# Both products of a feed-forward by seven block products, accumulated on one another in PSUM, with the activations' factors parked in DRAM

## The chip, the core and the metric

One core of one Trainium2 chip runs the program. The metric is the device time of one execution in microseconds, as the median of several runs. The profile is of one further execution; its engines are TensorE (PE, with PEld for its weight loads), VectorE (DVE), ScalarE (ACT), GpSimd (POOL) and SyncE (SP, whose queue issues the DMAs).

## What is computed

A trunk of two encoder layers on two requests, 512 and 256 tokens, with 1024 channels. Each layer is a mixer, a cross attention into a memory of 256 tokens, and a gated feed-forward with 2816 inner channels:

```python
def trunk(x, mem, ...):
    for l in range(DEPTH):
        h = rms_norm(x, norm_mix[l])
        ...                                   # even: convolution and Fourier; odd: windowed means
        h = rms_norm(x, norm_xa[l])
        m = rms_norm(mem, norm_mem[l])
        x = x + memory_cross_attn(h, m, xa_wq[l], xa_wkv[l], xa_wo[l])
        h = rms_norm(x, norm_ffn[l])
        x = x + swiglu(h, ffn_w_gate_up[l], ffn_w_down[l])
    return rms_norm(x, norm_final)

def swiglu(h, w_gate_up, w_down):
    gu = h @ w_gate_up
    g, u = gu[..., :D_FF], gu[..., D_FF:]
    return (jax.nn.silu(g) * u) @ w_down
```

Everything is float32.

## The kernel before

The residual stream stays in SBUF for the whole program: eight tiles `x[k]` of 128 channels by 768 tokens. A product in float32 is three matmuls of operands with short mantissas: `split` writes a high part on ScalarE (L119, with a gain L122) and the rest on VectorE (L120, L123), and `prod` multiplies high by high, high by low and low by high. One unit of weights is fetched by SP into one of four tiles `raw` (L138) and split into `wh` and `wl` in a pool of seven.

The feed-forward (`ffn`) goes by chunks of 128 inner channels, 22 of them, in the groups (4, 4, 4, 5, 5). A group's chunks get their gates and values, then its down products are added to x (`residual`, L289). Tokens are handled as halves of 384, so that a matmul is 128x384.

- Chunks 0 to 3 are plain: `linear` for gates and for values, eight input chunks by two token halves by three matmuls each.
- Chunks 4 to 21 use Winograd's form of Strassen's product (`seven`): gates and values are the rows, the two halves of the input channels the inner blocks, the two halves of the tokens the columns. Seven block products of sums of blocks take the place of eight, 7 × 4 × 3 = 84 matmuls a chunk. `left_factors` makes the seven weights' sums and splits them; `right_factors` makes the sums of the normalised input once. The latter is a generator that `advance(rf, PRE)` drives piecewise beside plain chunks 2 and 3 and the first down product. VectorE adds the seven results into gates and values (L871, L872).
- All down products are plain, `linear` over the group's activations, which stay in SBUF.
- In layer 0's last group, `advance(beside, 2)` makes the memory's parts for the mixer of layer 1. In layer 1's last group the down product goes by two pieces of the tokens, so that the final norm of one runs beside the product of the other.

All tiles are in one set of pools for the whole program; each engine's order is the scheduler's, by these dependencies.

## Time and profile before

| | |
|---|---|
| Median of three runs | 1805.79 us (1805.6 to 1805.99) |
| Span of the profiled execution | 1803.7 us |
| TensorE busy | 1785.7 us, 99% |
| VectorE busy | 1311.6 us, 73% |
| ScalarE busy | 668.5 us, 37% |
| Moved by DMA | 130.33 MB, of which 3.15 MB written |

The page gives no time for the profiled execution beyond its span, which runs from its first to its last instruction; the median lies 2.1 us above it. A share on the page is a mean over stages of different kinds. In the rows of the prediction a group has its count, its busy time, the mean of one in ns, and the idle time of the engine ahead of it with what ended it; a row of a stretch has, after its length, each engine's busy time with its number of instructions, the granted clock of TensorE, the share of DMA and GB/s; a row of the chain or the timeline has start and duration in us.

### The profile page before, as it was taken

What the parts mean: (1) busy time and instruction counts of PE and PEld (TensorE: products, weight loads), DVE (VectorE), ACT (ScalarE), POOL (GpSimd) and SP (SyncE); (2) the same over time, 40 slices, a digit from 0 to 9 for tenths busy, and PEclk for the clock granted to TensorE, in tenths of its full rate; (3) what the DMA queues carried; (4) which work ended last, traced back from release to release, by engine and by line L of the source; (5) the groups of instructions that cost most, each with busy time, mean ns of one, the idle gap of its engine ahead of it and who ended that gap; (6) DMA issues with size and microseconds to landing.
All of it is one profiled execution on the core that took longest, in us unless ns stands there. A gap on an engine that the chain in (4) does not pass through costs nothing.

```text
span 1803.7 us, 26005 instructions
## 1 busy us (share of the span) xinstructions
PE 1785.7 (99%) x10606; PEld 1748.0 (97%) x10606; DVE 1311.6 (73%) x2083; ACT 668.5 (37%) x1049; POOL 2.5 (0%) x40
## 2 busy tenths in 40 slices
PE   9999999999999999999999999999999999999997
PEld 8999999999999999999999999999999999999996
DVE  7998976486787757585767984496697767684765
ACT  7233243353443424242345243362443323241341
POOL 0000000000000000000000000000000000000000
PEclk9999999999999999999999999999999999999999
DMA  7231321111112221222224231111113121222211
GB/s 250 82 116 55 95 67 54 47 36 59 53 30 94 59 82 54 87 66 63 71 60 128 82 104 60 36 49 57 47 36 95 57 83 53 87 63 68 78 52 70
DMA packets 44326, 130.33 MB, mean 72 GB/s; under 512 B 4912, under 2 KB 6192, under 8 KB 44208
## 3 DMA queue, kind: packets, MB, share of 16 engines
q1 hardware_dynamic: 44208, 128.68, 23.5%
q8 instruction: 83, 1.36, 0.3%
q14 instruction: 35, 0.29, 0.1%
HBM read 125.51 MB, written 3.15 MB: 71 GB/s over the span
## 4 chain that ended last, share of the span: by engine, by line
PE 97%; DVE 2%; DMA 0%; ACT 0%; SPq 0%; issue 0%; DVEq 0%; ACTq 0%
PE acc L155 97%; DVE s L120 1%; DMA x<-in_x 0%; PE acc L713 0%; DVE s L988 0%; DVE st L695 0%; ACT Rx L234 0%; DVE c L704 0%; DVE kl L120 0%; DVE s L662 0%; SPq L304 0%; DVE x L975 0%; DVE c L221 0%; DVE s L123 0%; ACT s L122 0%
## 5 line engine op out<-in xcount | busy, mean ns | idle before, releaser
L155 PE MATMUL acc<-s,wh 128*128 128x384 f32 (+1 forms) x3528 | 782.4, 339 | 5.1 <-ACT Rx L234 3.6
L155 PEld LDWEIGHTS acc<-s,wh 128*128 128x128 f32 x3528 | 624.6, 188 | 21.4 <-ACT Rx L234 6.1
L155 PE MATMUL acc<-s,w 128*128 128x384 f32 x3120 | 543.8, 334 | 0.0
L155 PEld LDWEIGHTS acc<-s,w 128*128 128x128 f32 x3120 | 541.0, 188 | 0.4
L155 PE MATMUL acc<-s,wl 128*128 128x384 f32 (+1 forms) x1764 | 466.6, 339 | 0.0
L155 PEld LDWEIGHTS acc<-s,wl 128*128 128x128 f32 x1764 | 319.1, 188 | 6.5 <-DVE wl L120 0.5
L119 ACT ACTIVATE wh<-raw 128x1024 fp32r<-128x1024 f32 (+3 forms) x179 | 155.3, 873 | 454.6 <-PE acc L155 427.1
L120 DVE TENSOR_TENSOR wl<-raw,wh 128x1024 fp32r<-128x1024 f32 (+3 forms) x177 | 175.5, 995 | 115.1 <-PE acc L155 87.2
L289 DVE TENSOR_TENSOR x<-acc,x 128x768 f32<-128x768 f32 x152 | 145.1, 956 | 134.5 <-PE acc L155 134.5
L871 DVE TENSOR_TENSOR c<-acc,c 128x384 f32<-128x384 f32 x252 | 133.3, 553 | 43.6 <-PE acc L155 28.3
L119 ACT ACTIVATE w<-raw 128x512 fp32r<-128x512 f32 x148 | 92.5, 630 | 171.9 <-PE acc L155 168.7
L119 ACT ACTIVATE w<-h 128x512 fp32r<-128x512 f32 x108 | 68.1, 632 | 177.9 <-PE acc L155 177.9
L155 PE MATMUL acc<-wh,s 128*128 128x256 f32 x704 | 129.0, 283 | 0.0
L120 DVE TENSOR_TENSOR w<-raw,w 128x512 fp32r<-128x512 f32 x148 | 101.3, 689 | 24.6 <-ACT w L119 24.6
L155 PEld LDWEIGHTS acc<-wh,s 128*128 128x128 f32 x704 | 110.6, 192 | 0.2
L120 DVE TENSOR_TENSOR w<-h,w 128x512 fp32r<-128x512 f32 x108 | 74.1, 687 | 38.3 <-ACT w L119 38.3
L119 ACT ACTIVATE s<-c 128x768 fp32r<-128x768 f32 (+1 forms) x92 | 68.2, 756 | 66.9 <-DVE c L919 19.5
L155 PE MATMUL acc<-wl,s 128*128 128x256 f32 x328 | 92.8, 283 | 0.0
L120 DVE TENSOR_TENSOR s<-c,s 128x768 fp32r<-128x768 f32 (+1 forms) x92 | 76.6, 853 | 15.8 <-ACT s L119 14.6
L155 PE MATMUL acc<-s,s 128*128 128x512 f32 (+3 forms) x492 | 86.6, 334 | 0.0
L155 PEld LDWEIGHTS acc<-s,s 128*128 128x128 f32 x492 | 75.8, 189 | 9.8
L395 DVE SCALAR_TENSOR_TENSOR c<-c,vec,c 128x392 f32<-128x392 f32 x124 | 70.5, 633 | 0.2
(132 smaller groups left out, 1241.7 us busy)
## 6 DMA issues: line engine op xcount, KB each, us to landing
raw<-in_wgu SPq DMA_DIRECT2D x88, 512.0 KB, 3.5
raw<-in_wd SPq DMA_DIRECT2D x48, 256.0 KB, 2.6
raw<-in_wd SPq DMA_DIRECT2D x32, 320.0 KB, 2.9
raw<-in_wk SPq DMA_DIRECT2D x16, 512.0 KB, 3.6
raw<-in_wv SPq DMA_DIRECT2D x16, 512.0 KB, 3.6
raw<-in_wq SPq DMA_DIRECT2D x16, 512.0 KB, 3.5
raw<-in_wo SPq DMA_DIRECT2D x16, 512.0 KB, 3.5
raw<-in_m SPq DMA_DIRECT2D x16, 256.0 KB, 2.7
```

Source lines behind the costliest of these rows:

```text
L119: nc.scalar.activation(hi, src, AF.Copy)
L120: nc.vector.tensor_tensor(lo, src, asf(hi), ALU.subtract)
L155: nc.tensor.matmul(o, a, b, start=start, stop=stop)
L289: nc.vector.tensor_tensor(two(x[d]), halves(ps), two(x[d]), ALU.add)
L395: nc.vector.scalar_tensor_tensor(out_, src[:, a : a + CL], w, prev, ALU.mult, ALU.add)
L871: add = lambda o, a, b: nc.vector.tensor_tensor(o, a, b, ALU.add)
```

## The change

- Chunks 0 and 1 stay plain; chunks 2 to 21 go by seven products.
- The down product goes by seven products too, for two chunks (a pair) and two blocks of 128 output channels at a time: `output_job`. Its groups count pairs: (2, 3, 3, 3) in layer 0, (2, 3, 4) in layer 1, whose last two pairs stay plain and go by pieces of the tokens as before. A group has four output jobs, with 42 matmuls per job for a group of two pairs, 63 for three and 84 for four.
- Both kinds of jobs run through one pipeline, `run`. Results P6, P5 and P3 are accumulated in PSUM on top of P1, and P4 on top of P7. P3 and P4 of a job are made between P1 and P5 of the next. A weight's factor (`left`) is made six products ahead; its sums are on VectorE (L871 to L877). PSUM tiles in the feed-forward are one bank each, eight of them.
- When a pair of chunks is done, `finished` makes its sums and parts at once and parks them in DRAM, 2.75 MB in four writes on SP's queue (`keep`, L921); layer 1's last two pairs write parts alone. `load` reads a group's factors back (L1051): for the first group in the last hidden job, for group g+1 ahead of the weights of group g's second job.
- The input's factors are all made behind the token scale R, around the sums of plain chunks 0 and 1 (`some_factors`, then `other_factors`, L984 and L814).
- The memory's parts for layer 1 are made at the start of `mixer_odd`.
- The pools of mixer and attention (`mixing`) and those of the feed-forward (`feeding`) are separate sets, opened and closed in turn on the same memory.

Line numbers move: `split` is L144 to L148, the fetch L163, the matmul L180, the residual add L320, sums of the feed-forward L813 and L814.

```diff
-GROUPS = (4, 4, 4, 5, 5)
-PLAIN = GROUPS[0]
-PRE = 3
+NPAIR = NF // 2
+GROUPS = ((2, 3, 3, 3), (2, 3, 4))
+AHEAD = 6
...
-    rawp = E(tc.tile_pool(name="rawp", bufs=4))
...
-    acc = E(tc.tile_pool(name="acc", bufs=4, space=bass.MemoryType.PSUM))
+    park = E(tc.tile_pool(name="park", bufs=1, space=bass.MemoryType.DRAM))
...
+            pool = lambda name, bufs, **k: s.enter_context(tc.tile_pool(name=name, bufs=bufs, reuse_waits="tile", **k))
+            rawp, wp, hp, cp, sp = pool("rawp", 4), pool("wp", 7), pool("hp", 3), pool("cp", 8), pool("sp", 19)
+            acc = pool("acc", 4, space=bass.MemoryType.PSUM)
+            yield
...
+            f = SimpleNamespace()
+            rawp, wp, f.sum, f.pair, f.t2 = pool("raw2", 4), pool("wp2", 7), pool("sum", 2), pool("pair", 2), pool("t2", 4)
+            cp, sp = pool("cp2", 4), pool("sp2", 18)
+            acc = pool("acc2", 8, space=bass.MemoryType.PSUM)
+            yield f
...
-    def mixer_odd(l, o, ms):
+    def mixer_odd(l, o):
         hs = split_x(x, "mix", l)
-        ks, vs = [], []
+        ms, ks, vs = [], [], []
+        advance(memory_parts(l, ms), KD)
...
+        def first_factors(r, spare):
+            s1 = duo_split(r[:, 0::2, :])
+            t13 = chunk()
+            sub(two(t13), r[:, 1::2, :], r[:, 0:2, :])
+            s2 = duo_split(two(t13))
+            t2 = fp.t2.tile([P, H], F32, tag="t2", name=nm("t2"))
+            sub(t2, r[:, 3, :], t13[:, :H])
+            th = next(spare)
+            split(th[:, :H], th[:, H:T], t2)
+            return s1, s2, th, t2
...
+        def left(job, role):
+            n = job.cols
+            if role == "P1":
+                if job.before is not None:
+                    job.before()
+                job.a1, job.a2 = [fetch(src, 2 * n) for src in job.src]
+                a21, a22 = job.a2[:, :n], job.a2[:, n : 2 * n]
+                job.s1, job.s2 = [fp.sum.tile([P, 512], F32, tag="sum", name=nm("sum"))[:, :n] for _ in range(2)]
+                put(job, role, job.a1[:, :n])
+                WSUM(job.s1, a21, a22, ALU.add)
+                WSUM(job.s2, job.s1, job.a1[:, :n], ALU.subtract)
+                WSUM(a21, job.a1[:, :n], a21, ALU.subtract)
+            elif role == "P2":
+                a12 = job.a1[:, n : 2 * n]
+                put(job, role, a12)
+                WSUM(a12, a12, job.s2, ALU.subtract)
+            else:
+                src = {"P6": job.s2, "P7": job.a2[:, :n], "P5": job.s1, "P3": job.a1[:, n : 2 * n], "P4": job.a2[:, n : 2 * n]}
+                put(job, role, src[role])
+        def product(job, role):
+            home = {"P6": "P1", "P5": "P1", "P3": "P1", "P4": "P7"}.get(role)
+            if home is None:
+                job.bank[role] = bank()[:, :H]
+            o = job.bank[home or role]
+            w = job.w.pop(role)
+            m = len(job.right)
+            for k, right in enumerate(job.right):
+                prod([o], cut(w, slice(k * P, (k + 1) * P)), [right[role]], k == 0 and home is None, k == m - 1, home is not None)
+            for f in job.on[role]:
+                f(o)
+        def run(jobs):
+            seq, prev = [], None
+            for job in jobs:
+                for role in ("P1", "P2", "-P3", "P6", "-P4", "P7", "P5"):
+                    if role[0] != "-":
+                        seq.append((job, role))
+                    elif prev is not None:
+                        seq.append((prev, role[1:]))
+                prev = job
+            seq += [(prev, "P3"), (prev, "P4")]
+            for i in range(-AHEAD, len(seq)):
+                if i + AHEAD < len(seq):
+                    left(*seq[i + AHEAD])
+                if i >= 0:
+                    product(*seq[i])
...
+    def finished(q, pt):
...
+            d = parked[q] = park.tile([P, 3 * SLOT + T], F32, tag=f"pk{l}_{q}", name=f"pk{l}_{q}")
+            r = four(pt)
+            s1, s2, th, t2 = first_factors(r, spare)
+            sub(r[:, 1, :], r[:, 2, :], t2)
+            s4 = duo_split(r[:, 1::2, :])
+            for i, s in enumerate((s1, s2, s4)):
+                keep(d[:, i * SLOT : (i + 1) * SLOT], s)
+            keep(d[:, 3 * SLOT :], th)
...
+        some_factors(0)
+        act(0, *p0)
+        for k in range(1, M):
+            some_factors(k)
+        act(1, pg, plain(1, 1))
+        right = [other_factors(k) for k in range(M)]
...
+        def load(g):
+            back = lambda t, q, a, n: nc.sync.dma_start(t.bitcast(F32), parked[q][:, a : a + n])
+            got = {}
+            for i in (0, 3, 1, 2):
+                for q in groups[g]:
+                    if i == 3:
+                        t = next(spare)
+                        back(t, q, 3 * SLOT, T)
+                    else:
+                        t = slot()
+                        back(t, q, i * SLOT, SLOT)
+                    got[q, i] = t
+            loaded[g].extend(right_of(got[q, 0], got[q, 1], got[q, 3], got[q, 2]) for q in groups[g])
...
+            on = {
+                "P1": [to(x0, t0)], "P2": [to(x0, t0)], "P6": [to(x1, t0)], "P7": [lambda o: setattr(st, "b", o)],
+                "P5": [on_p5], "P3": [to(x0, t1)], "P4": [to(x1, t0)],
+            }
+            src = wd[l, at : at + P * 4 * n * P].rearrange("(p c) -> p c", p=P)
+            before = None
+            if j == 1 and g + 1 < len(groups):
+                before = lambda: load(g + 1)
...
+        jobs = [hidden_job(f) for f in range(2, NF)]
+        jobs[-1].on["P2"].append(lambda o: load(0))
+        at = 0
+        for g in range(len(groups)):
+            loaded[g] = []
+            for j in range(KD // 2):
+                jobs.append(output_job(g, j, at))
+                at += P * 4 * len(groups[g]) * P
...
-        ffn(l, memory_parts(nxt, ms) if nxt < DEPTH and nxt % 2 else None, nxt == DEPTH)
+        with feeding() as fp:
+            ffn(l, fp, l + 1 == DEPTH)
```

Three places in the order, names with the number of their tile.

VectorE, end of layer 0's attention and start of the feed-forward. `x0` to `x7` are the residual stream, `s` the split input. Before, the end of the last residual adds:

```order
L289 TENSOR_TENSOR x3_107<-acc_478_4297,x3_107 128x768
L123 SCALAR_TENSOR_TENSOR s_488_4379<-x2_106,vec_79,s_488_4379 128x768
L289 TENSOR_TENSOR x4_108<-acc_482_4317,x4_108 128x768
L123 SCALAR_TENSOR_TENSOR s_489_4382<-x3_107,vec_79,s_489_4382 128x768
L289 TENSOR_TENSOR x5_109<-acc_483_4331,x5_109 128x768
L123 SCALAR_TENSOR_TENSOR s_490_4385<-x4_108,vec_79,s_490_4385 128x768
L289 TENSOR_TENSOR x6_110<-acc_484_4345,x6_110 128x768
L123 SCALAR_TENSOR_TENSOR s_491_4388<-x5_109,vec_79,s_491_4388 128x768
L289 TENSOR_TENSOR x7_111<-acc_485_4359,x7_111 128x768
L123 SCALAR_TENSOR_TENSOR s_492_4391<-x6_110,vec_79,s_492_4391 128x768
```

Now, from the add to x6 on:

```order
L320 TENSOR_TENSOR x6_98<-acc_483_4351,x6_98 128x768
L320 TENSOR_TENSOR x7_99<-acc_484_4365,x7_99 128x768
L148 SCALAR_TENSOR_TENSOR s_485_4409<-x0_92,vec_63,s_485_4409 128x768
L148 SCALAR_TENSOR_TENSOR s_486_4412<-x1_93,vec_63,s_486_4412 128x768
L148 SCALAR_TENSOR_TENSOR s_487_4415<-x2_94,vec_63,s_487_4415 128x768
L148 SCALAR_TENSOR_TENSOR s_488_4418<-x3_95,vec_63,s_488_4418 128x768
L148 SCALAR_TENSOR_TENSOR s_489_4421<-x4_96,vec_63,s_489_4421 128x768
L148 SCALAR_TENSOR_TENSOR s_490_4424<-x5_97,vec_63,s_490_4424 128x768
L148 SCALAR_TENSOR_TENSOR s_491_4427<-x6_98,vec_63,s_491_4427 128x768
L148 SCALAR_TENSOR_TENSOR s_492_4430<-x7_99,vec_63,s_492_4430 128x768
L145 TENSOR_TENSOR wl_495_4436<-raw_493_4433,wh_494_4435 128x1024
```

The eight splits stood between the adds; now they, and the first weight's low part `wl_495` behind them, follow the last one.

VectorE, layer 0's feed-forward, from the first use of R (`Rx`) for the input's factors. Before:

```order
L816 SCALAR_TENSOR_TENSOR c_532_4686<-x0_104,vec_79,Rx_521_4611 128x768
L794 TENSOR_TENSOR c_530_4680<-c_530_4680,c_529_4677 128x768
L816 SCALAR_TENSOR_TENSOR c_533_4687<-x4_108,vec_79,Rx_521_4611 128x768
L872 TENSOR_TENSOR c_536_4698<-c_532_4686 128x384
L120 TENSOR_TENSOR s_531_4683<-c_530_4680,s_531_4683 128x768
L120 TENSOR_TENSOR s_534_4690<-c_532_4686,s_534_4690 128x384
L120 TENSOR_TENSOR s_534_4690<-c_533_4687,s_534_4690 128x384
L120 TENSOR_TENSOR s_535_4695<-c_533_4687,s_535_4695 128x384
L872 TENSOR_TENSOR c_536_4698<-c_533_4687,c_536_4698 128x384
L872 TENSOR_TENSOR c_537_4699<-c_533_4687,c_532_4686 128x384
```

Now (`pair_525` holds two scaled input chunks, `pair_532` the activations of chunks 0 and 1):

```order
L984 SCALAR_TENSOR_TENSOR pair_525_4654<-x0_92,vec_63,Rx_521_4645 128x768
L984 SCALAR_TENSOR_TENSOR pair_525_4654<-x4_96,vec_63,Rx_521_4645 128x768
L969 TENSOR_TENSOR pair_532_4671<-acc_501_4495,Rx_521_4645 128x384
L814 TENSOR_TENSOR c_527_4660<-pair_525_4654 128x768
L145 TENSOR_TENSOR s_526_4657<-pair_525_4654,s_526_4657 128x768
L814 TENSOR_TENSOR t2_529_4665<-pair_525_4654,c_527_4660 128x384
L145 TENSOR_TENSOR s_528_4662<-c_527_4660,s_528_4662 128x768
L145 TENSOR_TENSOR s_530_4667<-t2_529_4665,s_530_4667 128x384
L966 TENSOR_TENSOR c_531_4670<-acc_496_4439,Rx_521_4645 128x384
L966 TENSOR_TENSOR c_531_4670<-acc_497_4440,Rx_521_4645 128x384
```

Before, the factors of one pair of input chunks come behind the sums of two plain chunks, the next pair's after further plain work; now the four pairs follow one another from the first row on, 64 rows to the last split of P4's factors.

SP, layer 0, where the output products begin. Before, the first down products' weights and, among them, those of the next chunk:

```order
L138 DMA raw_600_5146<-in_wd 128x512
L138 DMA raw_604_5178<-in_wd 128x512
L138 DMA raw_608_5210<-in_wgu 128x1024
L138 DMA raw_609_5212<-in_wgu 128x1024
L138 DMA raw_615_5223<-in_wd 128x512
L138 DMA raw_620_5260<-in_wd 128x512
```

Now, the last eight of the twenty loads of parked factors (`pk0_2` is pair 2 of layer 0) and what follows them:

```order
L1051 DMA s_968_7642<-pk0_3_5743 128x768
L1051 DMA s_969_7645<-pk0_4_6023 128x768
L1051 DMA s_970_7647<-pk0_2_5462 128x1536
L1051 DMA s_971_7649<-pk0_3_5743 128x1536
L1051 DMA s_972_7651<-pk0_4_6023 128x1536
L1051 DMA s_973_7653<-pk0_2_5462 128x1536
L1051 DMA s_974_7655<-pk0_3_5743 128x1536
L1051 DMA s_975_7657<-pk0_4_6023 128x1536
L163 DMA raw_976_7659<-in_wd 128x512
L163 DMA raw_977_7661<-in_wd 128x512
```

Twenty loads, those of groups 0 and 1, stand ahead of `raw_976` and `raw_977`, the weights of the second output job.

More of the change, by code (lines that the diff above doesn't have):

```diff
@@ L1 @@
-from contextlib import ExitStack
+from contextlib import ExitStack, contextmanager
+from types import SimpleNamespace
 import numpy as np
@@ new lines, in ffn, with piece @@
+        jobs[-3].on["P1"].append(lambda o: load_acts())
+        run(jobs)
+        ws = []
+        for d in range(KD):
+            src = wd[l, at : at + P * gn * P].rearrange("(p c) -> p c", p=P)
+            at += P * gn * P
+            if d < 2:
+                ws.append(unit(src, gn * P))
+            else:
+                p = cut(pair(), slice(0, gn * P))
+                split(p[0], p[1], fetch(src, gn * P))
+                ws.append(p)
+        def piece(ds, tb, sq, late):
+            n = tb.stop - tb.start
+            ps = [bank()[:, :n] for d in ds]
+            for ks_ in (range(gn - 1), (gn - 1,)):
+                for d, p in zip(ds, ps):
+                    for k in ks_:
+                        prod([p], cut(ws[d], slice(k * P, (k + 1) * P)), [cut(acts[k], tb)], k == 0, k == gn - 1)
+            for d, p in zip(ds, ps):
+                nc.vector.tensor_tensor(x[d][:, tb], p, x[d][:, tb], ALU.add)
+                q = chunk()[:, :n]
+                nc.scalar.activation(q, x[d][:, tb], AF.Square)
+                if 1 <= d < late:
+                    add(sq[0], sq[0], q)
+                else:
+                    sq.append(q)
@@ L1021, in _constants @@
+        scaled(tb, row_of(token_root(sq, SS, 1.0 / D, RMS_EPS), SS))
+    for l in range(DEPTH):
+        with mixing():
+            if l % 2 == 0:
+                ks, vs = mixer_even(l, l // 2, loads() if l == 0 else [])
+            else:
+                ks, vs = mixer_odd(l, l // 2)
+            attention(l, ks, vs)
+        with feeding() as fp:
+            ffn(l, fp, l + 1 == DEPTH)
 def _constants():
```

448 lines of the change are left out of this document (215 added, 233 removed).

## The prediction

> **What bounds the kernel now.** I read the engines' shares first, then the chain, then stretches of the span, and last single instructions.
>
> ```profile
> span 1803.7 us, 26005 instructions
> PE 1785.7 (99%) x10606; PEld 1748.0 (97%) x10606; DVE 1311.6 (73%) x2083; ACT 668.5 (37%) x1049; POOL 2.5 (0%) x40
> PE 97%; DVE 2%; DMA 0%; ACT 0%; SPq 0%; issue 0%; DVEq 0%; ACTq 0%
> 432.02 65.10 PE acc L155 x376
> 498.00 624.86 PE acc L155 x3656
> 1300.57 483.41 PE acc L155 x2771
> ```
>
> TensorE is busy 99% and has 97% of the chain. The piece at 432 runs from the output product of layer 0's attention into the feed-forward without a break; the one at 498 runs through the feed-forward and on through the next mixer. There is no stall to win back: a gain can come only from fewer matmuls, and every new wait of TensorE is a loss. VectorE has 27% to spare, but that is an average; where the block products begin it is 79% busy (95.25 of 120 us, second row here):
>
> ```profile
> core 0: us, PE busy (x) PEld busy (x) DVE busy (x) ACT busy (x) POOL busy (x), PEclk, DMA share, GB/s
> 442.00:475.00 33.00, 33.00 (x193) 32.74 (x192) 25.53 (x28) 17.91 (x21) 0.00 (x0) 1.00 0.16 49
> 520.00:640.00 120.00, 120.00 (x692) 119.58 (x691) 95.25 (x146) 44.94 (x71) 0.00 (x0) 1.00 0.23 67
> 965.00:990.00 25.00, 25.00 (x143) 24.61 (x143) 17.97 (x21) 13.40 (x17) 0.37 (x6) 1.00 0.36 112
> ```
>
> **The gain: fewer matmuls.** The pace, from two rows of the steady part:
>
> ```profile
> 640.97 0.85 PE L155 MATMUL acc<-s,wh 128*128 128x384 f32 x4
> ...
> 652.40 0.85 PE L155 MATMUL acc<-s,wh 128*128 128x384 f32 x4
> ```
>
> Eleven sets of six lie between these starts: 11.43 us / 66 = 0.173 us each. A chunk costs 96 matmuls plain and 84 by seven products; its down product costs 48 plain, and by seven products a pair of chunks costs 84. Layer 0: before 4×96 + 18×84 + 22×48 = 2952, now 2×96 + 20×84 + 11×84 = 2796. Layer 1, whose last four chunks stay plain: 2×96 + 20×84 + 9×84 + 4×48 = 2820. That is 156 + 132 = 288 fewer, **-50 us**. Accumulating a role on another's bank takes VectorE sums away and adds no matmul.
>
> **Prices of VectorE.** Instructions of one queue overlap at their ends, so a run of several gives the pace:
>
> ```profile
> 527.21 2.69 DVE L120 TENSOR_TENSOR s<-c,s 128x768 fp32r<-128x768 f32 x3
> 529.82 1.95 DVE L816 SCALAR_TENSOR_TENSOR c<-x,vec,Rx 128x768 f32<-128x768 f32 x2
> 525.81 1.49 DVE L872 TENSOR_TENSOR c<-c,c 128x384 f32<-128x384 f32 x3
> 570.10 1.28 DVE L120 TENSOR_TENSOR w<-h,w 128x512 fp32r<-128x512 f32 x2
> 947.85 1.41 DVE L123 SCALAR_TENSOR_TENSOR s<-raw,vec,s 128x512 fp32r<-128x512 f32 x2
> L120 DVE TENSOR_TENSOR wl<-raw,wh 128x1024 fp32r<-128x1024 f32 x97 | 118.5, 1225 | 92.8 <-PE acc L155 79.6 <-issue 12.1 <-ACT c L415 0.7
> L120 DVE TENSOR_TENSOR s<-s,s 128x256 fp32r<-128x256 f32 x32 | 12.8, 419 | 0.0
> ```
>
> Start to start, after the about 0.08 us of overlap that these runs show: 0.87 us (768 columns), 0.93 (768 with a gain), 0.47 (384), 0.61 (512), 0.67 (512 with a gain), 1.14 (1024), 0.34 (256).
>
> In the steady part TensorE stays the bound: a chunk gives it 84 × 0.173 = 14.6 us, and VectorE seven splits and four sums of 512 (11 × 0.61), three sums of 384, a product of 768 and half of a pair's factors (4.9 us): 11.4 us. So these sums cost nothing there, nor do the parked writes: they move 2.75 MB per 29 us, 95 GB/s more. An output job of two pairs has 42 matmuls, 7.3 us, against 11 × 0.34 + 7 × 0.47 = 7.0 of VectorE; that is no cover, and I take 3 us of waits per layer for the four such jobs: **+6** (0 to 15).
>
> **1. Attention to feed-forward, both layers.** Before, the splits of the normalised input stand between the residual adds that produce x, while the output product still runs:
>
> ```profile
> 459.15 0.96 DVE L289 TENSOR_TENSOR x<-acc,x 128x768 f32<-128x768 f32 x1 [0.30 <-PE acc L155]
> 460.02 1.01 DVE L123 SCALAR_TENSOR_TENSOR s<-x,vec,s 128x768 fp32r<-128x768 f32 x1
> 460.95 1.22 DVE L120 TENSOR_TENSOR wl<-raw,wh 128x1024 fp32r<-128x1024 f32 x1
> 462.09 0.95 DVE L289 TENSOR_TENSOR x<-acc,x 128x768 f32<-128x768 f32 x1
> ```
>
> Now the eight splits and the first weight's low part follow the last add: 8 × 0.93 + 1.14 = 8.6 us. TensorE can start four matmuls before it needs that low part; their 0.7 us goes against the 1 us of the last add. Nothing else is in its queue: **+17** for both layers (bounds 5, if the first chunks' splits were early, to 20).
>
> **2. Head of the feed-forward, both layers.** Before, the input's factors were made beside plain chunks 2 and 3 and the first down product. Now they stand in one run behind the token scale R, with the sums of the first two plain chunks. VectorE's order from the first scaled x to the last P4 factor: 12 × 0.93 + 22 × 0.87 + 24 × 0.47 + 6 × 0.61 = 45.3 us. TensorE's matmuls between R and the one that reads this factor are 152: 26.4 us. It is late by 19 us at least, and up to 27 where ScalarE's high copies, waiting on the same sums, delay VectorE; I take 23: **+46** (20 to 54).
>
> **3. Load burst where the output products begin, both layers.** The queue of SP is in order, and the factors of the first two groups, 5.5 + 8.3 = 13.8 MB, are all issued ahead of the weights of the second output job. Before has no such burst; its densest stretch is the start:
>
> ```profile
> 10.00:15.00 5.00, 4.91 (x27) 4.60 (x28) 5.00 (x6) 5.00 (x7) 0.00 (x0) 1.00 1.05 403
> raw<-in_wd SPq DMA_DIRECT2D x48, 256.0 KB, 2.6
> raw<-in_m SPq DMA_DIRECT2D x16, 256.0 KB, 2.7
> out_y<-s SPq DMA_DIRECT2D x2, 768.0 KB, 3.4
> ```
>
> At 403 GB/s 13.8 MB take 34 us, with the weight's own landing (2.6) and the wait for slots that the last hidden products free, 36 to 43. The first of the loads may go after P2 of the last hidden chunk; from there TensorE has 124 matmuls, 21.5 us. Late by 15 to 21 us per layer, 18 taken: **+36** (20 to 50). The Trainium skill, "DMA: Bandwidth & Descriptors", section Specifications, limits a core's HBM traffic to about 358 GB/s; the 403 of this row is above that. By the page the burst would be an estimated 38.5 us and the sum 9 us higher.
>
> Later groups do the same with less: a load of up to 8.3 MB (20 us) stands ahead of the second job's weights, where the slots let it. Two places per layer, 3 to 5 us each beyond the 82 or so matmuls (14 us) of cover: **+14** (0 to 30).
>
> **4. Feed-forward of layer 0 to the mixer.** The memory's splits (L123) were made beside the last down products, one is the row at 947.85 above. They now come behind the last add, with the input's own: 8 × 0.93 + 8 × 0.67 = 12.8 us, and twice a landing of 2.7, since memory and pool weights share four raw tiles which the splits free: **+18** (8 to 22), once.
>
> **The sum**: -50 + 6 + 17 + 46 + 36 + 14 + 18 = +87 on the span of 1803.7: 1891. The median of the runs, 1805.79, lies 2.1 above this span: 1893. The terms 2 and 3 may share some waiting with what precedes them, so I say 1890. Startup and tail change little (0 taken, ±3).
>
> **Rivals.**
>
> Loads hidden: if the transfers run ahead of TensorE, or the order on SP is kinder than I read it, terms 3 and its later cases fall away: 1890 - 50 = 1840. For it: DMA is busy 23% in the steady part. Against: the loads wait for slots that only the last products free. Chance 0.17.
>
> Faster: TensorE's buffered work covers both loads and head. The head decides: it would have to be spread by the waits themselves, with TensorE taking the factors one by one as they come, so that VectorE's 45 us lie beside 26 us of plain work and 20 of products. Then terms 1 and 4 alone remain, -50 + 35 = -15: 1791; with these covered too, 1756. It turns faster once all waits together are under 50 us. Against it: 45.3 us exceed 26.4 by rows alone, twice. Chance 0.1.
>
> Longer waits: the clock falls in them. The end of before shows it, when TensorE runs dry:
>
> ```profile
> 1790.00:1794.00 4.00, 2.62 (x22) 2.45 (x21) 3.85 (x9) 0.84 (x2) 0.00 (x0) 1.00 0.61 239
> 1794.00:1798.00 4.00, 0.92 (x4) 0.62 (x4) 2.68 (x13) 0.00 (x0) 0.00 (x0) 0.82 0.56 219
> 1798.00:1804.00 6.00, 0.00 (x0) 0.00 (x0) 2.37 (x7) 0.00 (x0) 0.00 (x0) 0.50 0.50 175
> ```
>
> It goes from 1.00 to 0.50 within about 4 us. I count some 11 waits that long (two each at places 1, 2 and 3, one at 4, four later). If each is followed by up to 4 us at half the pace, that is 11 × 2 = 22 us: 1912, and 1926 with 50 for place 3. No row shows a restart after such a wait, so the sum has none of it. The Trainium skill, "TensorE: Matmul & The Clock Gate", Part 1, has the clock halved after an idle window of about 3.4 us and restored after as long a busy one: an estimated 1.7 us each, 19 in all, hence 1909; the fall in these rows agrees with it. Chance 0.13.
>
> **Chances and range.** The forecast as summed 0.57, with its own range 1860 to 1910; loads hidden 0.17; longer waits 0.13; faster 0.1; within 0.2% (about what this measurement tells from no change) 0.03. Range 1835 to 1925: it takes in the loads hidden and the fallen clock, and leaves out the faster cases and the far end.
>
> **What would show it.** In the trace after: some 10230 matmuls; TensorE's share near 92%; idle time of TensorE ended by the split of the gain (L148) or a weight's low part (L145) at both attention ends; 20 us in a few gaps behind R, ended by splits (L145) on VectorE or ScalarE; a stretch of some 35 us near 400 GB/s where the output products begin, with TensorE waiting for a weight behind it; one gap of 18 us before the mixer; the clock below 1.00 in slices with gaps, if the last rival holds. It is wrong if the head's gaps are under 10 us, or the bursts are over before TensorE has used its first output weights.

## The result, and the profile after

The changed kernel takes 1917.8 us (median of four runs, 1917.3 to 1918.0) against 1805.9 for the kernel before on the same chip: 1.062 times the time, 95% interval 1.060 to 1.063. The profiled execution spans 1915.4 us, 111.7 more than before's 1803.7.

From the page of the kernel after: the span, the engines' busy time, the granted clock in 40 slices, and the chain's shares.

```profile
span 1915.4 us, 26643 instructions
PE 1778.5 (93%) x10314; PEld 1726.9 (90%) x10314; DVE 1448.8 (76%) x2439; ACT 781.5 (41%) x1351; POOL 2.5 (0%) x40
PEclk9999999999879999978998999999879999988999
PE 85%; DVE 8%; DMA 5%; ACT 1%; issue 0%; SPq 0%; DVEq 0%; ACTq 0%
```

TensorE has 292 matmuls fewer and is busy 7 us less, but its share fell from 99 to 93%, and 13% of the chain is now VectorE and DMA. The clock row shows where: two dips at the attentions' ends and heads (slices 11 and 12, 29 and 30), and dips where output products run (18, 19 and 36, 37) and at the mixer (22).

Where the time lies, by stretches of the kernel after (columns as in the prediction):

```profile
core 0: us, PE busy (x) PEld busy (x) DVE busy (x) ACT busy (x) POOL busy (x), PEclk, DMA share, GB/s
470.00:480.00 10.00, 2.35 (x7) 1.63 (x8) 10.00 (x11) 6.71 (x8) 0.00 (x0) 0.68 0.00 0
480.00:507.00 27.00, 27.00 (x151) 27.00 (x151) 16.67 (x30) 6.31 (x9) 0.00 (x0) 0.93 0.24 78
507.00:554.00 47.00, 34.54 (x131) 29.26 (x129) 46.21 (x66) 25.31 (x38) 0.00 (x0) 0.71 0.18 69
554.00:822.00 268.00, 268.00 (x1546) 267.57 (x1545) 220.27 (x346) 141.65 (x259) 0.00 (x0) 1.00 0.47 164
822.00:860.00 38.00, 16.34 (x92) 16.02 (x92) 11.11 (x21) 4.69 (x11) 0.00 (x0) 0.77 0.98 391
860.00:903.00 43.00, 34.29 (x183) 32.80 (x183) 32.16 (x74) 13.22 (x31) 0.00 (x0) 0.90 0.66 244
903.00:955.00 52.00, 45.75 (x253) 45.34 (x252) 36.11 (x73) 13.78 (x28) 0.00 (x0) 0.93 0.63 228
1034.00:1059.00 25.00, 7.41 (x31) 6.60 (x30) 18.34 (x23) 16.49 (x22) 0.18 (x3) 0.66 0.40 136
1342.00:1352.00 10.00, 1.95 (x8) 1.04 (x7) 9.77 (x11) 8.42 (x11) 0.00 (x0) 0.77 0.01 2
1352.00:1381.00 29.00, 29.00 (x154) 28.64 (x155) 17.58 (x31) 7.19 (x11) 0.00 (x0) 0.90 0.23 73
1381.00:1427.00 46.00, 31.75 (x128) 26.89 (x126) 45.74 (x66) 24.45 (x37) 0.00 (x0) 0.78 0.18 72
1700.00:1726.00 26.00, 11.14 (x63) 10.82 (x63) 5.70 (x12) 2.32 (x6) 0.00 (x0) 0.74 0.90 365
1726.00:1768.00 42.00, 33.84 (x183) 33.00 (x181) 30.92 (x73) 11.80 (x28) 0.00 (x0) 0.91 0.64 231
1768.00:1897.00 129.00, 127.50 (x708) 123.07 (x709) 91.19 (x173) 39.84 (x72) 0.00 (x0) 0.98 0.36 129
```

Reading: the stretch from 554 gives the pace without a wait, 268.00 / 1546 = 0.1734 us a matmul. A stretch's length less its matmuls at this pace is what it loses. (Busy PE won't do: at half clock it counts as busy.)

| place | stretches from | lost, us | predicted, us |
|---|---|---|---|
| attention to feed-forward | 470, 480; 1342, 1352 | 9.6 + 10.9 = 20.5 | 17 |
| head of the feed-forward | 507; 1381 | 24.3 + 23.8 = 48.1 | 46 |
| first load burst | 822; 1700 | 22.0 + 15.1 = 37.1 | 36 |
| later groups' loads | 860, 903; 1726, 1768 | 19.4 + 16.5 = 35.9 | 14 |
| mixer of layer 1 | 1034 | 19.6 | 18 |

Together 161.2; less the 50 of fewer matmuls this is +111.2, against the 111.7 between the spans. The sum takes every matmul as one of 128x384, so it is good to a microsecond or two; it leaves no more than that for the rest of the program.

The chain of work names the waits. Pieces of it at layer 0's attention end, first burst and later loads, and then TensorE's rows behind its four waits there:

```profile
473.38 4.73 DVE s L148 x5
478.11 1.15 DVE wl L145
...
823.50 8.31 DMA s<-pk
831.83 13.93 DMA s<-pk
845.82 12.88 DMA raw<-in_wd
...
892.39 9.49 DMA raw<-in_wd
...
945.92 8.25 DMA raw<-in_wd
```

```profile
479.30 1.00 PE L180 MATMUL acc<-s,wl 128*128 128x384 f32 x2 [4.28 <-DVE wl L145]
859.25 27.67 PE L180 MATMUL acc<-s,w 128*128 128x384 f32 x146 [21.66 <-ACT w L144]
902.56 46.04 PE L180 MATMUL acc<-s,w 128*128 128x384 f32 x252 [8.25 <-ACT w L144]
954.86 5.33 PE L180 MATMUL acc<-s,w 128*128 128x384 f32 x20 [6.25 <-ACT w L144]
```

At 473 the chain goes through five of the eight gain splits and then the first weight's low part; at 823 through the parked factors and then the weights behind them; at 892 and 945 through weights that took 9.5 and 8.3 us to land. SP's issues show why they were late: loads of parked factors stand ahead of them (`x20` are those of groups 0 and 1; the weights of 845.82 and 892.39 come directly behind these two runs):

```profile
819.51 25.66 SPq L1051 DMA_DIRECT2D s<-pk  x20
882.52 9.77 SPq L1051 DMA_DIRECT2D s<-pk  x8
```

In the head, VectorE runs from the first scaled x to the last P4 factor almost without a pause (46.2 of the 47 us from 507). The first row and the last:

```profile
509.41 1.94 DVE L984 SCALAR_TENSOR_TENSOR pair<-x,vec,Rx 128x768 f32<-128x768 f32 x2
554.10 0.95 DVE L145 TENSOR_TENSOR s<-c,s 128x768 fp32r<-128x768 f32 x1
```

From 509.41 to 555.05 are 45.6 us (45.3 in the sum), in which TensorE starts 125 matmuls. Its longest wait there is not for a split:

```profile
548.88 4.36 PE L180 MATMUL acc<-s,w 128*128 128x384 f32 x14 [5.89 <-ACT c L1012]
```

L1012 is ScalarE's copy of a job's P1 out of PSUM. Because P6, P5 and P3 are accumulated on top of P1, they must come behind it. ScalarE stood idle for 0.82 us ahead of this copy until a split on VectorE (L145) ended; in the code the copy needs one of four `chunk` tiles, which the factors use too. So the wait goes back to VectorE, by way of a tile; the same wait in layer 1 is 6.98 us. No run tried more of these tiles.

Ahead of the mixer stands one wait:

```profile
1053.98 3.88 PE L180 MATMUL acc<-s,w 128*128 128x384 f32 x12 [17.41 <-ACT w L144]
```

The granted clock in the trace is 1.00 or 0.50 and nothing between; where a stretch has a value between, it mixes the two. It stands at 0.50 in 13 stretches behind or in waits, and once more at the end of the span. The first two of the 13, and their sum:

```profile
473.60:483.90 10.30, 5.30 (x16) 4.89 (x16) 10.09 (x11) 6.00 (x8) 0.00 (x0) 0.50 0.28 98
521.40:541.90 20.50, 15.82 (x44) 13.28 (x45) 20.22 (x29) 9.78 (x14) 0.00 (x0) 0.50 0.04 15
...
sum 150.00, PE 70.02 PEld 64.40 DVE 101.60 ACT 61.45 POOL 0.00; mean PE 5.39 PEld 4.95 DVE 7.82 ACT 4.73 POOL 0.00
```

All 13 hold 209 matmuls, which at 0.173 would take 36.2 us and took 70.0: 33.8 us more, of which 16.7 in the heads, where VectorE is behind anyway, and 17.1 elsewhere. These 33.8 us are inside the losses of the table, not beside them. That the 16.7 cost nothing by themselves is argued from VectorE's full rows, not tried.

### The profile page after: what moved, and what is told of

The parts are those of the page before. It is cut to its first block, busy times and chain, and to the rows that moved or that the text cites. A ratio compares the mean times of both kernels' runs of the same rounds, so it can differ in the third digit from the quotient of the medians.

```text
span 1915.4 us, 26643 instructions
## 1 busy us (share of the span) xinstructions
PE 1778.5 (93%) x10314; PEld 1726.9 (90%) x10314; DVE 1448.8 (76%) x2439; ACT 781.5 (41%) x1351; POOL 2.5 (0%) x40
## 3 DMA queue, kind: packets, MB, share of 16 engines
q1 hardware_dynamic: 66096, 245.08, 37.1%
## 4 chain that ended last, share of the span: by engine, by line
PE 85%; DVE 8%; DMA 5%; ACT 1%; issue 0%; SPq 0%; DVEq 0%; ACTq 0%
PE acc L180 85%; DMA raw<-in_wd 3%; DVE s L145 2%; DMA s<-pk 2%; DVE s L148 1%; DVE pair L984 1%; DVE c L814 1%; DVE w L145 0%; DVE c L984 0%; ACT w L144 0%; DMA x<-in_x 0%; DVE s L1149 0%; PE acc L748 0%; DMA raw<-in_wk 0%; DVE t L814 0%
## 5 line engine op out<-in xcount | busy, mean ns | idle before, releaser
L180 PE MATMUL acc<-s,w 128*128 128x384 f32 x5136 | 928.6, 342 | 104.1 <-ACT w L144 77.9
L180 PEld LDWEIGHTS acc<-s,w 128*128 128x128 f32 x5136 | 912.7, 193 | 118.6 <-ACT w L144 80.7
L180 PE MATMUL acc<-s,wh 128*128 128x384 f32 (+1 forms) x2016 | 463.6, 345 | 10.9 <-ACT wh L144 8.0
L180 PEld LDWEIGHTS acc<-s,wh 128*128 128x128 f32 x2016 | 360.6, 189 | 26.7 <-ACT wh L144 10.0
L144 ACT ACTIVATE w<-raw 128x512 fp32r<-128x512 f32 (+2 forms) x344 | 196.3, 579 | 359.6 <-PE acc L180 242.5
L145 DVE TENSOR_TENSOR w<-raw,w 128x512 fp32r<-128x512 f32 (+2 forms) x344 | 211.5, 624 | 102.4 <-ACT w L144 97.7
L180 PE MATMUL acc<-s,wl 128*128 128x384 f32 (+1 forms) x1008 | 277.6, 344 | 8.3 <-DVE wl L145 8.3
L180 PEld LDWEIGHTS acc<-s,wl 128*128 128x128 f32 x1008 | 184.5, 190 | 15.1 <-DVE wl L145 9.6
L144 ACT ACTIVATE wh<-raw 128x1024 fp32r<-128x1024 f32 (+2 forms) x99 | 98.7, 1005 | 218.1 <-PE acc L180 201.8
L145 DVE TENSOR_TENSOR wl<-raw,wh 128x1024 fp32r<-128x1024 f32 (+2 forms) x97 | 112.2, 1164 | 71.0 <-PE acc L180 52.5
L813 DVE TENSOR_TENSOR x<-acc,x 128x384 f32<-128x384 f32 x196 | 107.4, 553 | 48.9 <-PE acc L180 47.3
L180 PE MATMUL acc<-wh,s 128*128 128x256 f32 x704 | 129.0, 284 | 0.0
L320 DVE TENSOR_TENSOR x<-acc,x 128x768 f32<-128x768 f32 x80 | 76.2, 955 | 49.1 <-PE acc L180 49.1
L180 PEld LDWEIGHTS acc<-wh,s 128*128 128x128 f32 x704 | 110.7, 192 | 0.2
L145 DVE TENSOR_TENSOR w<-sum,w 128x512 fp32r<-128x512 f32 (+2 forms) x136 | 84.8, 623 | 28.9 <-ACT w L144 28.2
L144 ACT ACTIVATE w<-sum 128x512 fp32r<-128x512 f32 (+2 forms) x136 | 78.5, 577 | 61.9 <-PE acc L180 31.0
L180 PE MATMUL acc<-wl,s 128*128 128x256 f32 x328 | 92.9, 283 | 0.0
L180 PE MATMUL acc<-s,s 128*128 128x512 f32 (+3 forms) x456 | 80.6, 335 | 0.0
L180 PEld LDWEIGHTS acc<-s,s 128*128 128x128 f32 x456 | 70.3, 190 | 9.5 <-issue 0.5
L813 DVE TENSOR_TENSOR pair<-acc,c 128x384 f32<-128x384 f32 x80 | 44.4, 555 | 42.1 <-ACT c L1025 25.9
L180 PEld LDWEIGHTS acc<-wl,s 128*128 128x128 f32 x328 | 62.9, 192 | 0.2
```

Of the source, the lines that this page charges most:

```text
L144: nc.scalar.activation(hi, src, AF.Copy)
L145: nc.vector.tensor_tensor(lo, src, asf(hi), ALU.subtract)
L180: nc.tensor.matmul(o, a, b, start=start, stop=stop, skip_group_check=more)
L320: nc.vector.tensor_tensor(two(x[d]), halves(ps), two(x[d]), ALU.add)
L813: add = lambda o, a, b: nc.vector.tensor_tensor(o, a, b, ALU.add)
```

## The experiments

The theory: five groups of waits, each with a cause of its own in the order of the work, and a fallen clock behind each. The main rival: the waits are one another's cover, so that taking one away only shows the next. The first nine runs below take the places one at a time, each as a change to the kernel after (1917.8 us).

**The first weight ahead of the splits** (attention to feed-forward).

```diff
+        ready = [unit(wgu[l, 0, 0])]
         hs = split_x(x, "ffn", l)
         def plain(f, j):
-            w = unit(wgu[l, f, j])
+            w = ready.pop() if ready else unit(wgu[l, f, j])
```

> The first gate weight of each feed-forward is fetched and split ahead of the input's eight splits; nothing else changes. In the changed kernel TensorE stands at 470 to 479 us for its low part, which comes behind the splits. Theory (VectorE's order at this place is the wait): the first weight's low part comes one instruction after the last residual add, and TensorE then follows the splits one by one, 0.93 us of VectorE against 1.04 of TensorE each; the 9 us wait falls to about 3 in both layers, and the time by 12 to 16 us, to 1902 to 1906. Rival (the memory of the closed pools is what comes free late): the wait stays 8 us or more, and the time within 3 us of 1917.8.

1905.1 us, 12.7 less than after (1.055 of before, 1.053 to 1.056). TensorE in that place waits 2 us for the first split and 0.75 for the second, no longer for the weight's low part behind all eight:

```profile
471.89 0.62 PE L180 MATMUL acc<-s,wh 128*128 128x384 f32 x2 [2.02 <-ACT s L147]
```

So the place of one weight's fetch and split ahead of eight others is worth 12.7 of the 20.5 us lost here. The rival of waits that cover one another is not without its part: if one sets the times of the same matmuls in both traces side by side, this place gave back 6.1 us in layer 0 and 7.0 in layer 1, and the heads behind it took 3.0 and 2.1 of that again. (The profiled execution was, with 1908.7, the slowest of the four.)

**R one plain product earlier** (head).

```diff
-        p0 = plain(0, 0), plain(0, 1)
+        p0 = [plain(0, 0)]
         r = token_root(square_sum(x), T, 1.0 / D, RMS_EPS)
-        pg = plain(1, 0)
+        p0.append(plain(0, 1))
...
             nc.scalar.activation(R[:, t], o, AF.Copy)
+        pg = plain(1, 0)
```

> The squares' sum, the token root and R are written behind the first of three plain products (instead of the second and third), so that up to 96 matmuls, 16.7 us, of plain work move behind R. Theory (the head is VectorE's 45 us of factors against 26 us of TensorE's work behind R): R comes some 14 us earlier and the waits of the head shrink by 12 to 15 us in each layer; time 1888 to 1895, and 1884 if the clock stays up as well. Rival (the factors wait for memory that the plain products' input gives back, 8 of 18 slots): the last factors come at the same distance from the last plain product, and the time stays within 5 us of 1917.8.

1908.8 us, 9.0 less (1.056, 1.055 to 1.058), about a third of the 23 to 30 that were expected and more than the rival's 5. VectorE's first scaled x starts at 501.4 instead of 509.4, since R's own matmuls stand behind plain(0, 1) in TensorE's queue; the factors then take 45 us again:

```profile
500.00:547.00 47.00, 33.29 (x163) 30.61 (x162) 47.00 (x68) 23.96 (x37) 0.00 (x0) 0.89 0.15 59
```

VectorE is busy all 47 us, which fits that its work bounds the head. But a start that is 8.0 us earlier did not gain 8.0: TensorE comes to the first load burst 3.7 us earlier (833.9 instead of 837.6), and 3.3 more are gained in layer 1's head. The wait for ScalarE's copies is still there (6.55 us), and a second one of 1.89 is new; why the other half of the earlier start was lost was not tried.

**A job's weights ahead of the next group's load.**

```diff
             if role == "P1":
+                job.a1, job.a2 = [fetch(src, 2 * n) for src in job.src]
                 if job.before is not None:
                     job.before()
-                job.a1, job.a2 = [fetch(src, 2 * n) for src in job.src]
```

> A job's own weights are fetched ahead of the load that goes with it; the same bytes in the same groups. Theory (the order on SP's queue is the wait): the second output job of a group finds its weights, and only the third waits behind the load, with one job more of cover, 7.3 us for a group of two pairs and 10.9 for three. The waits of 21.7, 8.3 and 6.3 us in layer 0 and 14.9 and 8.5 in layer 1 become about 13, 0, 0 and 6, 0, so 40 us less, with the clock 43: time 1875 to 1880. Rival (the transfers' rate is the bound, whatever the order): the waits move to the third job and to the next group's first factors in the same length, and the time stays above 1907.

1879.1 us, 38.7 less (1.040, 1.038 to 1.042), as the theory has it. TensorE's waits in layer 0's output products, two of seven:

```profile
861.83 20.52 PE L180 MATMUL acc<-s,w 128*128 128x384 f32 x104 [13.07 <-ACT w L144]
...
901.47 44.14 PE L180 MATMUL acc<-s,w 128*128 128x384 f32 x252 [0.59 <-DVE w L145]
```

The waits of 8.25 and 6.25 us at the later groups are gone; in the first burst one of 13.07 is left of 21.66. The order on SP's queue alone, with the same bytes moved, was worth 38.7 us. Matmul by matmul the trace has 11.4 of it in the two first bursts and 26.3 at the later loads, so not all of the table's 35.9 came back there.

**Small groups, their loads in three pieces behind the weights.**

```diff
-GROUPS = ((2, 3, 3, 3), (2, 3, 4))
+GROUPS = ((2, 2, 2, 2, 3), (2, 2, 2, 3))
...                                    # weights ahead of the load, as above
-            if j == 1 and g + 1 < len(groups):
-                before = lambda: load(g + 1)
+            if j > 0 and g + 1 < len(groups):
+                before = lambda: load(g + 1, ((0,), (3, 1), (2,))[j - 1])
```

> Groups of two pairs (2, 2, 2, 2, 3 in layer 0 and 2, 2, 2, 3 in layer 1) in place of (2, 3, 3, 3) and (2, 3, 4), so that two groups' factors fit into the slots at once; the next group's factors are loaded in three pieces behind the weights of jobs 2, 3 and 4. The bytes are the same. Theory (burst and order, not the amount): all five waits behind loads go, 60 us, and 6 to 8 of half clock with them; time 1848 to 1856. Jobs of two pairs cost little, since TensorE did not wait in those of the changed kernel. Rival (the amount of traffic, or VectorE in the small jobs of 7.3 us): waits of 3 us or more in each of the 36 output jobs, and a time above 1890.

1867.8 us, 50.0 less (1.034, 1.032 to 1.036): less than the theory's 62 to 70, far from the rival. All waits of TensorE for a weight's high part (total, count, longest), which were 77.9, 8 and 21.7 us in the kernel after:

```profile
PE acc L180 <- ACT w L144: 25.3, 9, 17.8
```

The longest is the mixer's. So the load waits are 7.5 us now instead of some 60; of the 73 us of the table's third and fourth rows 23 did not come back; some went into waits of under 1 us for VectorE, which has 144 more instructions (L145 and L813 end them).

**Twenty matmuls of ones by x in the wait at each attention's end,** computing nothing that is used.

```diff
+        idle = bank()[:, :H]
+        for _ in range(20):
+            mm(idle, ones, x[KD - 1][:, :H], True, True)
         p0 = plain(0, 0), plain(0, 1)
```

> Twenty matmuls whose result is used by nobody (ones times the last residual tile, in float32, 0.36 us each by those that make R) are put ahead of the first plain product of each feed-forward, so that TensorE is busy for some 7 of the 9 us that it waits there. Theory (a wait of more than some 4 us drops TensorE's clock to half, and the work after it pays): the half-clock stretches at 474 to 484 us and 1347 to 1358 go, and with them 2.5 and 3.1 us that 16 and 19 matmuls took too long; time 4 to 6 us lower, 1912 to 1914. Rival (the time at half clock costs nothing, since VectorE is behind anyway): time within 2 us of 1917.8, or above it by what the added matmuls outlast the wait.

1923.5 us, 5.7 more (1.065, 1.063 to 1.067). They took 13.2 us, 0.66 each, and each has two records:

```profile
470.70 13.17 PE L180 MATMUL acc<-x,ones 128*128 128x384 f32 x40 [1.05 <-DVE x L320]
```

The waits they stand in hold 8; the useful products go on at 483.42, 4.1 us later than the 479.30 of the kernel after. The clock was 1.00 throughout this place, but the run can't tell the clock's price from its own overrun.

**Ten of them.** The same edit with `range(10)`.

> As the kernel after, with ten matmuls of ones by x put into the wait of 8 us at each attention's end (the run with twenty kept the clock at 1.00 there, but took 13.2 us where 8.3 us were free). Ten at 0.66 us take 6.6 us and fit in the wait. Theory (the half-paced stretch that follows a wait is a cost of its own): the stretches of half clock behind these two waits, which held 2.5 and 3.1 us of excess, are gone and the next product keeps its place, 1912 to 1914 us, 4 to 6 below 1917.8. Rival (the work behind the wait is bound by VectorE's head, so an earlier start is only waited away there): 1916 to 1919.

1910.5 us, 7.3 less (1.058, 1.056 to 1.059), a little more than expected. The stretch behind the first attention:

```profile
468.00:480.00 12.00, 10.15 (x40) 6.86 (x40) 10.66 (x12) 7.71 (x10) 0.00 (x0) 1.00 0.00 1
480.00:507.00 27.00, 27.00 (x156) 26.14 (x157) 18.37 (x32) 7.89 (x12) 0.00 (x0) 1.00 0.24 78
```

The clock is 1.00 where it was 0.68 and 0.93, with 156 matmuls in the same 27 us instead of 151. The half-paced stretches behind these two waits had 2.5 + 3.1 us of excess: the clock behind a long wait is a cost of its own, and filling the wait takes it away. Up to the load bursts the trace has 1.7 us of gain in layer 0 and 2.8 in layer 1, so most of the 5.6 comes through the heads. The rest of the 7.3 came at waits behind loads, which were up to 1.5 us shorter; they differ by as much in runs that change nothing there (at layer 1's burst 14.86 us in the kernel after, 13.72 with the keys first, below).

**Memory and keys ahead of the input's splits** (mixer).

```diff
     def mixer_odd(l, o):
-        hs = split_x(x, "mix", l)
         ms, ks, vs = [], [], []
         advance(memory_parts(l, ms), KD)
         kv = keys_values(l, ms, ks, vs)
+        advance(kv, 2)
+        hs = split_x(x, "mix", l)
```

> In the mixer of layer 1 the memory's parts and the first head's keys are written ahead of the input's splits, so that TensorE can begin with the keys. Theory (VectorE's sixteen splits in a row and what they hold back are the wait of 17.4 us there): TensorE waits 7 to 8 us for the memory's eight splits (8 times 0.67, and the first key weight) and some 3 us once more for the first of the input's; time 8 to 12 us lower, 1906 to 1910. Rival (the loads into the four raw tiles are the wait): the memory's parts are no earlier, and the time stays within 4 us of 1917.8.

1915.3 us, 2.5 less (1.061, 1.059 to 1.063): the rival, and hardly to be told from no gain, since its runs lie 7.6 us apart. The wait goes only from 17.4 to 11.4 us, with another of 2.7 behind it, because the key weight comes behind eight memory blocks that share four raw tiles:

```profile
1049.62 1.22 PE L180 MATMUL acc<-s,wh 128*128 128x512 f32 x2 [11.41 <-ACT wh L144]
```

**Two input splits and two products first, two memory blocks to a raw tile.**

```diff
     def mixer_odd(l, o):
-        hs = split_x(x, "mix", l)
+        hs = split_x(x, "mix", l, ks=range(2))
...
-        advance(memory_parts(l, ms), KD)
...
-        ps = [product(units[0], *jobs[0])]
+        ps = [product(units[0], *jobs[i]) for i in range(2)]
+        advance(memory_parts(l, ms, True), KD)
         advance(kv)
+        hs += split_x(x, "mix", l, ks=range(2, KD))
```

> As the kernel after, with the start of layer 1's mixer in another order: two of the eight input splits and the 24 matmuls that read them come ahead of the memory's parts, two memory blocks share a raw tile, and two products are under way instead of one. The run with the memory's parts alone first gained 2.5 us and showed why: a weight that comes tile by tile behind the memory's raw tiles. Theory (the raw tiles and the splits' place together make the gap of 19.6 us): gap 5 to 9 us, 1904 to 1908 us. Rival (TensorE has nothing else than these parts to start on, so their splits set the start in any order): gap 15 us or more, 1913 to 1918.

1905.9 us, 11.9 less (1.055, 1.054 to 1.057), as the theory has it. The wait is two of 3.00 and 2.43 us, with 24 matmuls between them, partly at half clock (6.02 us where 4.2 would do):

```profile
1040.46 6.02 PE L180 MATMUL acc<-s,w 128*128 128x384 f32 x24 [3.00 <-ACT w L144]
1048.91 0.74 PE L180 MATMUL acc<-s,wh 128*128 128x512 f32 x2 [2.43 <-ACT wh L144]
```

**Four plain chunks at the head, as before, and R inside the second plain product.** Chunks 2 and 3 are plain again (48 more matmuls, 8.3 us), and the first two pairs are finished and parked later, in the first hidden jobs.

```diff
+        p0.append(plain(0, 1, make_R))         # R's matmuls ahead of its last two input chunks
+        pg = plain(1, 0)
...
         act(1, pg, plain(1, 1))
+        for k in range(2, M):
+            some_factors(k)
+        act(2, plain(2, 0), plain(2, 1))
+        act(3, plain(3, 0), plain(3, 1))
...
+        jobs = [hidden_job(f) for f in range(4, NF)]
+        for q in range(2):
+            jobs[q].on["P2"].append(lambda o, q=q: finished(q, pairs.pop(q)))
```

> Four plain chunks in place of two in each layer (2 x 2 x 12 = 48 matmuls more, 8.3 us), with R's matmuls in the middle of the second plain product, the first two pairs' sums put off behind the input's factors; the 45 us of factors then have some 75 us of TensorE's work beside them. Theory (VectorE's 45 us behind R): the head's waits fall from 24 us with the clock to 4 to 8 per layer; time 24 to 32 us lower after the cost, 1886 to 1894. Rival (slots: the plain input holds 8 of 18 and the factors need 14, so the last must wait for the last plain product whatever the number of chunks): the waits stay above 15 us per layer, and the time is 1908 or more.

1874.7 us, 43.0 less (1.038, 1.036 to 1.040), 11 to 19 us better than expected. Where the factors end now:

```profile
545.00:570.00 25.00, 25.00 (x146) 25.00 (x145) 24.92 (x40) 15.84 (x27) 0.00 (x0) 1.00 0.42 155
```

VectorE is as full as before, but TensorE has no wait there, from 482 to 600. All 48.1 us of the head came back, and 8.3 were paid for it; the remaining 3 us of gain are about what its runs lie apart (1873.8 to 1876.4).

**Four together:** first weight, four plain chunks, small groups in pieces, keys first.

> The first weight ahead (e1), four plain chunks with R in the middle of the second product (e7), groups of two pairs loaded in pieces (e4) and keys first (e6), together. If the waits are separate causes, their gains add up: 1917.8 less 12.7 (measured), 50 (measured), 28 and 10 (expected) is 1817; 1808 to 1828. If they share one cause, VectorE's total work say, what one frees another takes back, and the time stays above 1840.

1831.5 us, 86.3 less (1.013, 1.012 to 1.015), just beyond what was expected. Alone the four gave 12.7 + 43.0 + 50.0 + 2.5 = 108.2. 12.6 of the missing 22 us are a wait that alone was 1.4 us a layer in the run with the first weight ahead, and none in the others:

```profile
490.86 2.72 PE L180 MATMUL acc<-ones,c 128*128 128x1 f32 x12 [5.72 <-DVE c L276]
```

With the plain products starting earlier, the token root's matmuls, placed after the first of them, wait for the sum of squares on VectorE (5.7 us here, 6.9 in layer 1).

**With the token root behind both first plain products, and the mixer's second order.**

```diff
-        p0 = [plain(0, 0)]
+        p0 = plain(0, 0), plain(0, 1)
         r = token_root(square_sum(x), T, 1.0 / D, RMS_EPS)
...
-        p0.append(plain(0, 1, make_R))
-        pg = plain(1, 0)
+        pg = plain(1, 0, make_R)
```

> The earlier combination (first weight before the splits, four plain chunks at the head, small groups loaded in three pieces behind the weights, 1831.5 us) with the token scale's matmuls moved behind both first plain products, since they held TensorE 5.7 and 6.9 us there, and with the mixer's new order. Theory (waits are what costs, one by one): 1831.5 - 12.6 - some 8 to 10 at the mixer - up to 4 of clock = 1804 to 1812 us, level with the kernel before or just above. Rival (a wait taken away returns at the next load or split): above 1820. Faster than before (below 1802) would need the load bursts gone too, which nothing here changes.

1804.3 us, 0.999 of before (0.998 to 1.000), at the near end of what was expected: level with the kernel before. From its page:

```profile
PE 1762.3 (98%) x10362; PEld 1714.4 (95%) x10362; DVE 1453.0 (81%) x2551; ACT 768.0 (43%) x1371; POOL 2.5 (0%) x40
```

The end of layer 0's attention, and the first load burst:

```profile
470.00:480.00 10.00, 7.61 (x26) 6.82 (x25) 9.50 (x10) 9.63 (x12) 0.00 (x0) 0.66 0.19 52
815.00:840.00 25.00, 20.45 (x101) 18.86 (x102) 22.27 (x53) 9.38 (x25) 0.00 (x0) 0.93 0.93 358
```

The change had cost 111.9 us; its work in another order gave back 113.5, with 48 matmuls more. What the saved matmuls should give now, 50 - 8.3 = 42 us, still goes into smaller losses, 5.5 us in the first of these stretches and 7.5 in the second. Matmul by matmul against the kernel after, the output products keep some 19 us of the table's losses, the mixer 11, the attentions' ends 7 and the heads 3.

**The short waits that were left, filled too:** three matmuls of ones by x at each attention's end, four at the mixer, and there the first weight's split first.

```diff
     def mixer_odd(l, o):
-        hs = split_x(x, "mix", l, ks=range(2))
+        idle = big()[:, :H]
+        for _ in range(4):
+            mm(idle, ones, x[0][:, :H], True, True)
...
         units = [group(0)]
+        hs = split_x(x, "mix", l, ks=range(2))
...
+        idle = bank()[:, :H]
+        for _ in range(3):
+            mm(idle, ones, x[0][:, :H], True, True)
         ready = [unit(wgu[l, 0, 0])]
```

> The combination at 1804.3 us with the three short waits that it has left at the stages' borders filled: three matmuls of ones by x at each attention's end (2.0 us at 0.67 each, where the wait is 2.0 and 2.5 us), four at the start of layer 1's mixer (2.7 us, wait 3.0), and there the first weight's split ahead of the input's. They compute nothing that is used. Theory (the stretch of half clock behind a wait is a cost of its own, paid even behind waits as short as these): the half-paced stretches behind layer 0's attention and in the mixer go, and with them 1.7 us and 2.5 to 5 us: 1798 to 1801 us, faster than the kernel before by 0.3 to 0.4%. Rival (what these stretches hold back is made up, since VectorE sets the pace behind them): 1803 to 1806.

1804.6 us, 0.9987 of before (0.9978 to 0.9996): the rival's time. The clock was kept at 1.00 in the stretch from 470 to 480 that had 0.66, but at the mixer the next wait took over what was won:

```profile
994.23 0.73 PE L180 MATMUL acc<-s,wh 128*128 128x512 f32 x2 [2.77 <-ACT wh L144]
```

The first key product starts at 994.23, where it started at 994.12 without the filling: it waits for its own weight. At the attentions' ends products come about 1 us earlier, which the medians, whose runs lie 6 to 10 us apart, can't show. So behind short waits nothing measurable was to be had; whether the clock costs 1 or 2 us there stays open.

## Why the prediction was right, and where it was off

It said 1890 (1835 to 1925); the time is 1917.8, inside the range and outside the forecast's own 1860 to 1910. Sign and places were right. The size is that of the rival of longer waits, 1912 to 1926, which had a chance of 0.13; that this time came out is partly luck, since most of what the sum lacked came from one load term and not from the clock.

- **Fewer matmuls, -50.** 292 fewer records (10314; the "some 10230" of the prediction does not follow from its own 288, which give 10318); the 268 us stretch has the pace of before, without a wait, at VectorE 82% busy. That the steady part costs nothing held.
- **Attention to feed-forward, +17.** 20.5, by the wait named (L145 behind L148), as the run with the first weight ahead showed. The 3.5 above the term are within the excess of the half clock behind them, 2.5 + 3.1.
- **Head, +46.** 48.1. VectorE's run of 45.6 us against 45.3 in the sum is its closest step. The rows gave at least 19 us a layer; that 23 was taken out of 19 to 27 was a choice, and it fitted (24.3 and 23.8). The form of the waits was not all as said: those for splits are at most 2.2 us, and the longest, 5.89 and 6.98, for ScalarE's copy of P1, so that the accumulation in PSUM, which the prediction counted as sums saved, has a wait of its own here. The run with four plain chunks took the whole loss away; the one with R earlier gained a third of what VectorE's work as the only bound had promised.
- **First burst, +36.** 37.1, but by 22.0 and 15.1, of which the first lies outside the 15 to 21 a layer: the sum fits better than its parts. From the first load's issue to the weights' landing are 39.2 and 40.5 us, as reckoned (36 to 43); what differs is TensorE's cover, 18.1 and 26.2 instead of 21.5 in both. The Trainium skill, "DMA: Bandwidth & Descriptors", section Specifications, gives about 358 GB/s from HBM for a core; the 38 us stretch at 822 ran at 391, so the sum by the rate of before's densest row was the nearer one.
- **Later groups' loads, +14.** 35.9: this is the term that was mis-sized, and the 22 us are nearly all that the sum lacked. It allowed 3 to 5 us at each of two places per layer; the stretches lost 6.2 to 11.3. The waits are three, 8.25 and 6.25 us in layer 0 and 8.46 in layer 1, with 2.1, 1.5 and 2.6 us of half clock behind them. By the prediction's own numbers, 20 us of load less 14 of cover, a wait is 6 us and not 3 to 5. To this comes the landing of the weights themselves, which the first burst's term has with 2.6 us and this one leaves out; behind the loads it took 9.49, 8.25 and 9.72 us. The place and the cause were right: with the weights ahead of the loads these waits went. That the loads also started late, because SP waited 18.9 us in layer 0 and 9.4 in layer 1 for tiles that TensorE's products free, is read from the trace, not tried.
- **Mixer, +18.** 19.6, one wait of 17.4 as said.
- **Small output jobs, +6.** The table leaves at most a microsecond or two for them. In the run with small groups, which has 20 more of them, TensorE's waits for VectorE's sums and low parts (L813, L145) rose by 4.0 us in all, so their cover nearly held.
- **The clock, left to a rival.** That step was wrong as a decision: no row showed a restart, so the sum took nothing, but the fall was seen. It cost 17.1 us outside the heads, 1.5 to 3.1 a wait, where the rival said 2. The Trainium skill, "TensorE: Matmul & The Clock Gate", Part 1, has half or full clock only, in windows of about 3.4 us; the trace agrees (0.50 or 1.00, stretches of 6.8, 10.2, 17.0 and 20.4 us). Its estimate in the prediction, 1.7 us a wait and 19 in all, counted eleven waits with the heads' among them; on that count the trace has 33.8 in 13 stretches, and outside the heads 17.1 in eight, 2.1 each. Since the rival added this to a sum whose other terms held some of it, it is no separate +22 in the table.

## What to carry to other kernels

When a kernel has one engine at 99%, sum what each changed stage gives that engine to do while the others prepare; here five places in the order of work cost 161 us against 50 of saved matmuls, and nearly the same arithmetic (48 matmuls more) in another order took no longer than the kernel before. On a DMA queue that takes its transfers in order, issue what the next step needs ahead of bulk prefetch: one line moved was worth 38.7 us. A wait of several microseconds on TensorE cost a further 1.5 to 3.1 us at half clock here; at the attentions' ends, work put into it that fits, even useless, gave most of that back, while work that overran it cost more than it saved. Results that are accumulated on one another in PSUM save sums, but the first must be read before the next is added: where that read came late, in the heads, TensorE waited 5.89 and 6.98 us for it.

## What the hardware showed that was not expected

- A matmul of plain float32 operands took 0.66 us with two records (13.17 us for 20) where one of the split operands, of the same 128x384, takes 0.17.
- The clock stayed at 0.50 for 20.5 us where short waits, none above 1.93 us, followed one another (521.4 to 541.9 in the head), even though TensorE was busy for 15.8 of these 20.5 us, counted at half pace.
- The load burst held 391 GB/s for 38 us, close to the 403 of a 5 us stretch at the start of the kernel before.
